# A 256-token encoder layer on one core: q, f, b and up computed in channel rows

## The chip, the core and the metric

The kernel runs on one core of a Trainium2 chip. The core has five engines that work side by side and wait for one another by semaphores: TensorE (matrix products; a pass loads a stationary tile of weights, PEld, and then moves columns past it, PE), VectorE (DVE), ScalarE (ACT), GpSimd (POOL) and SyncE (SP, which here issues the transfers). TensorE writes to PSUM, an accumulator memory of eight banks of 512 fp32 words in each of 128 partitions; the other data lies in SBUF. The metric is the device time of one execution in microseconds, as a median over runs.

## The reference

One layer: a bidirectional HGRN2 mixer, then a gated ConvFFN, each between two RMS norms, on 256 tokens of 2048 channels.

```python
h = rmsnorm(x, norm_pre_mix)
q, f_f, f_b, v, g = split(h @ w_in)            # five parts of 2048 columns
q = silu(q); f = lb + (1 - lb) * sigmoid(f_raw); k = 1 - f
S_t = diag(f_t) S_{t-1} + k_t v_t^T;  o_t = S_t^T q_t      # both directions, 16 heads, summed
m = (rmsnorm(o, gnorm) * silu(g)) @ w_out
x = x + rmsnorm(m, norm_post_mix)
h = rmsnorm(x, norm_pre_ffn)
gate, val = split(dwconv3(h @ ffn_w_in))       # 2 x 5632 columns, filter of width 3 over tokens
x = x + rmsnorm((silu(gate) * val) @ ffn_w_out, norm_post_ffn)
```

## The kernel before

**Products.** Every product is split into chunks of 512 output columns: 20 of w_in (four heads' worth of q, f, b, g or v), 4 of w_o, 22 of w_up, 4 of w_dn. Each fp32 operand is split exactly into a high and a low part of type fp32r, and a product is the sum of high x high, high x low and low x high. The activations lie transposed in SBUF (xh and xl, later h2h and h2l: 16 row tiles of 128 channels by 256 tokens). `gemm` takes, for each of 16 row tiles and each of two blocks of 128 tokens, the block's tile of activations as stationary operand and 512 columns of weights as moving operand (lines 173, 176, 177): 16 x 2 x 3 = 96 passes of 512 columns a chunk. The two results, one bank each for 128 tokens x 512 channels, have the tokens in the partitions. A norm's factor per token (rs1, rs2) is there one number per partition, and is applied as the scale of the ScalarE instruction that reads the bank.

**Weights.** SP loads 1 MB at a time (`load`, line 116, three buffers); ScalarE rounds the high part out of it (line 130) and VectorE subtracts it for the low part (line 131), in parts of two row tiles, three parts ahead of TensorE (`prep`).

**Turning the results.** The gates, the scores and the filter over tokens want the channels in the partitions and the tokens along a row. So the chunks of q, f (forward), b (backward) and up are evicted (ScalarE and, for q, VectorE: lines 303, 304, 321, 594) and then turned by `two_tiles`: eight transposes of 128x128 on TensorE (line 196) into PSUM tiles named tp. What follows reads tp: the copy to qT (314), the forget gates (333), the filter (602, 607, 608). g, v, w_o and w_dn are used with the tokens in the partitions.

**Scores and rest.** `do_scores` makes the decayed scores of four heads in seven levels, with fp32 products of 128 columns (lines 374, 394, 419), VectorE and ScalarE working between levels; `do_o` makes the outputs. In the score of level i the moving operand is gathered in runs of 2^i words out of two arrays.

**What sets the order.** Such work is not done at once but put into lists (`soon`, `later`), and `gemm` takes one step of them after each part of a chunk. Within this, a scheduler orders each engine's instructions by a simulated time; an instruction under `keep_in_program_order` stays where the program has it in respect of others so marked and what precedes it. Each engine then runs its list in order. Four PSUM banks (tag pg) hold the results of two chunks at a time; two hold tp and two the scores.

**Start.** x is loaded in pieces of 256, 256, 512, 512 and 512 columns, in between the first weights; `split_x` transposes two row tiles of x at a time (line 257) and splits them. The mean square of x is taken during the second chunk, so rs1 is there before its results are evicted; rs2 is taken at the end of the first up chunk.

Of the kernel before, what the change touches and what calls it, by code (L numbers as in the profile page):

```python
# [18 lines left out]
P = 128  # L19
# [13 lines left out]
# the parts of the first projection, four heads at a time  # L33
# [3 lines left out]
# columns of the packed per-partition parameters  # L37
# [9 lines left out]
def encoder_layer(  # L47
# [34 lines left out]
    mk = const.tile([P, NLEV - 1, P], U8, name="mk")  # L82
# [51 lines left out]

    def flush():
        while soon or later:
            step()

    def gemm(xh, xl, order="plain", need=None, pre=None, mid=None):
# [16 lines left out]
        for s, m in seq:  # L156
            if s == need:
                flush()
            if pre and m == 0:
                pre(s)  # L160
            if order == "head" and s < 4:
                ahead = 4 + m * s
            elif order == "tail" and s >= nsub - 4 - LOOK:
                late = s - (nsub - 4)
                ahead = nsub + (min(0, 2 * late) if late < 0 else late + 1 if m == 0 else 4)
            else:
                ahead = s + (LOOK if ci else 1)
            prep(base + ahead)
            hi, lo = parts[ci, s]
            for j in range(2):  # L170
                k = 2 * s + j
                a, b = xh[:, k, m * P : (m + 1) * P], xl[:, k, m * P : (m + 1) * P]
                mm = nc.tensor.matmul(ps[m], a, hi[:, j, :], start=(k == 0), stop=False)  # L173
                if j == 0 and (order == "head" and s < 4 or order == "tail" and m == 1 and s >= nsub - 4):
                    tc.keep_in_program_order(mm)
                nc.tensor.matmul(ps[m], a, lo[:, j, :], start=False, stop=False)  # L176
# [5 lines left out]
        return ps  # L182

    def rsqrt_mean(dst, ss, n):
        V.tensor_scalar(dst, ss, 1.0 / n, EPS, op0=ALU.mult, op1=ALU.add)
        G.tensor_tensor(dst, dst, mneg[:, : dst.shape[1]], op=ALU.pow)
# [16 lines left out]
    # ------------------------------------------------------------- start up  # L203
    xh = acts.tile([P, KT, T], F32R, name="xh", tag="ah")
    xl = acts.tile([P, KT, T], F32R, name="xl", tag="al")
# [4 lines left out]
    mkf = spool.tile([P, NLEV - 1, P], F32, name="mkf")  # L210
# [17 lines left out]
    def load_rest():  # L228
        nc.sync.dma_start(prm[:, C_CW:], par[:, C_CW:])
        nc.sync.dma_start(mkf, masks.rearrange("p (l t) -> p l t", t=P))  # L230
        V.tensor_copy(mk, mkf)

    # the tensor engine reaches its full clock after some microseconds of work
# [4 lines left out]
    # lower bounds of the forget gates: softmax over the layers, cumulative  # L238
    # sum, minus the first layer's value
# [12 lines left out]
    def split_x(k2):  # L252
# [5 lines left out]
        for j in range(2):  # L258
            k = 2 * k2 + j
            w1 = prm[:, C_PRE + k : C_PRE + k + 1]  # L260
            S.activation(xh[:, k, :], tp[:, j, :], AF.Copy, scale=w1)
        for j in range(2):
# [3 lines left out]
                xl[:, k, :], tp[:, j, :], w1, xh[:, k, :].bitcast(F32), op0=ALU.mult, op1=ALU.subtract  # L266
# [16 lines left out]
    nop = lambda: None  # L283
# [8 lines left out]
    # ------------------------------------------------------- HGRN2, both ways  # L292
    opool = pool(hstack, "oacts", side="right")
    oh = opool.tile([P, KT, T], F32R, name="oh")
    ol = opool.tile([P, KT, T], F32R, name="ol")
# [11 lines left out]

    def do_q(g):
        ps = gemm(xh, xl) if g else ps0
        qn = [nat.tile([P, 512], F32, name="qn", tag="qn") for _ in range(2)]  # L310
        for m in range(2):
            silu_nat(ps, m, qn[m])
        qT = hp.tile([P, HG, T], F32, name="qT", tag="qT")
        two_tiles(lambda i, tp: S.copy(qT[:, 2 * i : 2 * i + 2, :], tp), qn)
        st["q", g] = qT

    def do_f(g, d):
        ps = gemm(xh, xl) if g or d else ps1
# [10 lines left out]
        def put(i, tp):  # L329
            for j in range(2):  # L330
                h = 2 * i + j
                c = d * NH + g * HG + h
                V.tensor_scalar(
                    f[:, h, :], tp[:, j, :], lb1[:, c : c + 1], lb[:, c : c + 1], op0=ALU.mult, op1=ALU.add
# [6 lines left out]
        two_tiles(put, sn, rest)  # L341
# [86 lines left out]
    def do_g(g):  # L428
        ps = gemm(xh, xl)
# [5 lines left out]
    def do_v(g):  # L435
        ps = gemm(xh, xl)
# [5 lines left out]
    def do_o(g):  # L442
# [23 lines left out]
        def put(i, tp):  # L466
            sl = slice(g * HG + 2 * i, g * HG + 2 * i + 2)
            S.activation(oh[:, sl, :], tp, AF.Copy, scale=gn)
            V.scalar_tensor_tensor(ol[:, sl, :], tp, gn, oh[:, sl, :].bitcast(F32), op0=ALU.mult, op1=ALU.subtract)
# [18 lines left out]
    # -------------------------------------------- output projection, residual  # L488
    ps0 = gemm(oh, ol, need=6)
# [10 lines left out]
    def project(xh_, xl_, sfx, ps0, wp, mw, jp, done):  # L500
        """The product of all columns, and the mean square of its rows."""
# [17 lines left out]
        for n in range(4):  # L519
            if n < 3:  # L520
                ps = ps0 if n == 0 else gemm(xh_, xl_)
                take(n, 0, ps)
            else:
                V.tensor_reduce(part, ss.rearrange("p (m q) -> p m q", q=4)[:, :, :3], axis=AX.X, op=ALU.add)
                V.tensor_scalar(part, part, 1.0 / D, EPS, op0=ALU.mult, op1=ALU.add)
                ps = gemm(xh_, xl_, "tail", mid=lambda ps: take(3, 0, ps))
            take(n, 1, ps)

    h2h = acts.tile([P, KT, T], F32R, name="h2h", tag="ah")
    h2l = acts.tile([P, KT, T], F32R, name="h2l", tag="al")  # L530
    ss2, sx2, rs2 = stile(8, "ss2"), stile(2, "sx2"), stile(2, "rs2")

    def mix_done(m, rs):
# [6 lines left out]
        def split(n):  # L540
# [5 lines left out]
            for j in range(4):  # L546
                k = 4 * n + j
                w1 = prm[:, C_PREF + k : C_PREF + k + 1]
                S.activation(h2h[:, k, ms], tp[:, j, :], AF.Copy, scale=w1)
            for j in range(4):  # L550
# [3 lines left out]
                    h2l[:, k, ms], tp[:, j, :], w1, h2h[:, k, ms].bitcast(F32), op0=ALU.mult, op1=ALU.subtract  # L554
# [19 lines left out]
    project(oh, ol, "m", ps0, wp, mw, bpool, mix_done)  # L574
    ps0 = gemm(h2h, h2l, "head")
# [8 lines left out]
    gh = gpool.tile([P, FT, T], F32R, name="gh")  # L584
    gl = gpool.tile([P, FT, T], F32R, name="gl")
# [4 lines left out]
    def up(c, done):  # L590
        ps = gemm(h2h, h2l) if c else ps0
        un = [fn.tile([P, 512], F32, name="un", tag="un") for _ in range(2)]
        for m in range(2):
            S.activation(un[m], ps[m], AF.Copy, scale=rs2[:, m : m + 1])
# [15 lines left out]
        two_tiles(put, un, lambda: done(acc))  # L610

    for j in range(NJ):
# [6 lines left out]
        def val_done(a, gate=gate, j=j):  # L619
            sl = slice(4 * j, 4 * j + 4)  # L620
            V.tensor_tensor(a, gate[0], a, op=ALU.mult)
            S.copy(gh[:, sl, :], a)
            V.tensor_tensor(gl[:, sl, :], a, gh[:, sl, :].bitcast(F32), op=ALU.subtract)
# [3 lines left out]
    ps0 = gemm(gh, gl, need=20)  # L627
# [14 lines left out]
    project(gh, gl, "f", ps0, wp2, fw, dpool, ffn_done)  # L642


def _masks():
# [3 lines left out]
    return mk.astype(np.float32).reshape(P, -1)  # L649
# [52 lines left out]
```

## Time and profile before

| What | us |
|---|---|
| Median of 3 runs (1385.96 to 1387.13) | 1386.12 |
| Span of the profiled execution | 1383.9 |
| TensorE busy in it | 1372.2 |
| VectorE busy | 862.4 |
| ScalarE busy | 684.1 |
| First to last chunk of w_up | 633.5 to 1135.4 |

The span runs from the first to the last instruction of one profiled execution; the runs are timed apart from it, and their median stands 2.2 us above it. A TensorE pass is shown from its start to the end of its results, and passes overlap, so that busy time says whether TensorE ever stood still, and the step from one start to the next says what a pass costs. In the timeline a row has start, length, engine, line, operation, output<-inputs, the moving shape and a count of merged instructions; what ended an idle time before it stands in brackets. In groups of instructions, the columns behind the bars are busy time, mean length and idle time before them with what ended it. The granted TensorE clock is full in the mean (0.998).

### The profile page before, as it was taken

Reading aid. Unit: us, or ns where it says so; the run is one execution under the profiler, and the core shown is the slowest. Engines: PE = TensorE matmul, PEld = TensorE weight load, DVE = VectorE, ACT = ScalarE, POOL = GpSimd, SP = SyncE. Lnnn points to the kernel's source line nnn. Section 1 sums busy time; section 2 is a strip of 40 time slices with the busy share of each in tenths; the row PEclk is TensorE's granted clock in tenths of the full one; section 3 lists DMA queues with packets and bytes.
Section 4 is the critical chain, followed back from the end, with each engine's and each line's share of the span. In section 5 each row is a group of like instructions: output and inputs, shape, how many; then the busy total and the mean of one; then the engine's idle time right before and its main releaser. Section 6 shows DMA issues by size and latency. Waiting matters only on the chain.

```text
span 1383.9 us, 16448 instructions
## 1 busy us (share of the span) xinstructions
PE 1372.2 (99%) x6562; PEld 1148.5 (83%) x6562; DVE 862.4 (62%) x1007; ACT 684.1 (49%) x899; POOL 13.5 (1%) x21
## 2 busy tenths in 40 slices
PE   8999999999999999999999999999999999999997
PEld 7888888888888888888888888888888888888886
DVE  6577657855785776567566565656566656444444
ACT  6644544444444445456555555555555554434342
POOL 0000000000000000000000000000000000000000
PEclk9999999999999999999999999999999999999999
DMA  8553454445444534663555555555555556555552
GB/s 315 183 188 125 149 174 164 149 140 182 165 152 153 174 130 159 242 255 105 188 197 181 194 182 183 183 182 183 185 184 186 184 192 225 186 199 193 185 205 97
DMA packets 36988, 249.08 MB, mean 180 GB/s; under 512 B 4144, under 2 KB 4784, under 8 KB 7472
## 3 DMA queue, kind: packets, MB, share of 16 engines
q1 hardware_dynamic: 36912, 248.04, 51.9%
q8 instruction: 51, 0.84, 0.2%
q14 instruction: 25, 0.20, 0.0%
HBM read 245.93 MB, written 2.10 MB: 179 GB/s over the span
## 4 chain that ended last, share of the span: by engine, by line
PE 98%; DMA 1%; issue 0%; SPq 0%; DVE 0%; ACT 0%; DVEq 0%; POOLq 0%; POOL 0%
PE pg L176 30%; PE pg L177 30%; PE pg L173 30%; PE sc L394 4%; PE tp L196 2%; DMA xs<-in_x 1%; PE sc L451 1%; PE sc L419 1%; PE sc L374 1%; PE sc L450 1%; PE tp L545 0%; PE tp L257 0%; DVE fw L639 0%; SPq L116 0%; SPq L213 0%
## 5 line engine op out<-in xcount | busy, mean ns | idle before, releaser
L131 DVE TENSOR_TENSOR wlo<-raw,whi 128x1024 fp32r<-128x1024 f32 (+1 forms) x457 | 557.2, 1221 | 426.1 <-ACT whi L130 425.7
L130 ACT CAST whi<-raw 128x1024 fp32r<-128x1024 f32 (+1 forms) x457 | 479.6, 1051 | 506.8 <-PE pg L177 486.9
L177 PE MATMUL pg<-whi,h2l 128*128 128x512 f32 x704 | 276.3, 392 | 0.0
L176 PE MATMUL pg<-wlo,h2h 128*128 128x512 f32 x704 | 276.2, 392 | 0.0
L173 PE MATMUL pg<-whi,h2h 128*128 128x512 f32 x704 | 276.1, 393 | 0.0
L173 PE MATMUL pg<-whi,xh 128*128 128x512 f32 x640 | 251.6, 395 | 0.0
L177 PE MATMUL pg<-whi,xl 128*128 128x512 f32 x640 | 251.4, 393 | 0.0
L176 PE MATMUL pg<-wlo,xh 128*128 128x512 f32 x640 | 250.9, 392 | 0.0
L177 PEld LDWEIGHTS pg<-whi,h2l 128*128 128x128 f32 x704 | 132.3, 188 | 28.3
L176 PEld LDWEIGHTS pg<-wlo,h2h 128*128 128x128 f32 x704 | 132.3, 188 | 26.2
L173 PEld LDWEIGHTS pg<-whi,h2h 128*128 128x128 f32 x704 | 132.2, 188 | 25.9
L177 PEld LDWEIGHTS pg<-whi,xl 128*128 128x128 f32 x640 | 120.2, 188 | 24.6
L176 PEld LDWEIGHTS pg<-wlo,xh 128*128 128x128 f32 x640 | 120.3, 188 | 23.4 <-DVE wlo L131 0.2
L173 PEld LDWEIGHTS pg<-whi,xh 128*128 128x128 f32 x640 | 120.3, 188 | 23.3
L177 PE MATMUL pg<-whi,gl 128*128 128x512 f32 x352 | 137.0, 389 | 0.0
L173 PE MATMUL pg<-whi,gh 128*128 128x512 f32 x352 | 137.0, 389 | 0.0
L176 PE MATMUL pg<-wlo,gh 128*128 128x512 f32 x352 | 137.0, 389 | 0.0
L176 PEld LDWEIGHTS pg<-wlo,gh 128*128 128x128 f32 x352 | 66.1, 188 | 13.8
L173 PEld LDWEIGHTS pg<-whi,gh 128*128 128x128 f32 x352 | 66.1, 188 | 13.7
L177 PEld LDWEIGHTS pg<-whi,gl 128*128 128x128 f32 x352 | 66.1, 188 | 13.6
L394 PEld LDWEIGHTS sc<-qs,kc 128*128 128x128 f32 x448 | 57.9, 192 | 2.2
L607 DVE SCALAR_TENSOR_TENSOR acc<-tp,prm,acc 128x255 f32<-128x255 f32 x88 | 41.8, 476 | 27.3 <-PE tp L196 27.3
(108 smaller groups left out, 1010.6 us busy)
## 6 DMA issues: line engine op xcount, KB each, us to landing
raw<-in_w_up SPq DMA_DIRECT2D x88, 1024.0 KB, 4.9
raw<-in_w_in SPq DMA_DIRECT2D x78, 1024.0 KB, 4.9
raw<-in_w_dn SPq DMA_DIRECT2D x44, 1024.0 KB, 4.9
raw<-in_w_o SPq DMA_DIRECT2D x16, 1024.0 KB, 4.9
x<-in_x SPq DMA_DIRECT2D x1, 2048.0 KB, 7.6
wp<-in_post SPq DMA_DIRECT2D x2, 1024.0 KB, 5.9
out<-fw SPq DMA_DIRECT2D x8, 256.0 KB, 2.5
xs<-in_x SPq DMA_DIRECT2D x3, 512.0 KB, 10.2
```

Of the source, the lines that this page charges most:

```text
L130: S.copy(hi[:, j], src[:, j])
L131: V.tensor_tensor(lo[:, j], src[:, j], hi[:, j].bitcast(F32), op=ALU.subtract)
L173: mm = nc.tensor.matmul(ps[m], a, hi[:, j, :], start=(k == 0), stop=False)
L176: nc.tensor.matmul(ps[m], a, lo[:, j, :], start=False, stop=False)
L177: nc.tensor.matmul(ps[m], b, hi[:, j, :], start=False, stop=(k == 2 * nsub - 1))
L196: nc.tensor.transpose(tp[:, j, m * P : (m + 1) * P], srcs[m][:, c0 : c0 + P], ident)
L374: nc.tensor.matmul(sc[:, j, :], kc[0][:, h, sl], q[:, h, sl], start=True, stop=True)
L394: nc.tensor.matmul(sc[:, j, :], kc[0][:, h, sl], r, start=True, stop=True)
L419: nc.tensor.matmul(sc[:, h, :], ks[:, d, h, s0 : s0 + P], qs[:, 1 - d, h, t0 : t0 + P], start=True, stop=True)
L450: nc.tensor.matmul(o[:, h, :], Sd[:, 2 * h + b, :], v[:, b, cs], start=True, stop=False)
L451: nc.tensor.matmul(o[:, h, :], So[1 - b][:, h, :], v[:, 1 - b, cs], start=False, stop=True)
L607: V.scalar_tensor_tensor(a[:, 1:T], z[:, 0 : T - 1], cw[0], a[:, 1:T], op0=ALU.mult, op1=ALU.add)
```

## The change

`gemm_t` is a second way to compute a chunk: the weights are the stationary operand, in four tiles of 128 columns, and the activations of all 256 tokens move. For each of 16 row tiles and each of the four column tiles there are three passes of 256 columns (lines 205, 208, 209 of the changed kernel): 192 a chunk. The result has the channels in the partitions and the tokens along a row, in two banks of two column tiles each. All q, f and b chunks and all up chunks but the first use it; g, v, the first up chunk, w_o and w_dn keep `gemm` (now lines 175, 178, 179).

With the tokens along the row, a norm's factor per token is no scale per partition any more. `spread` makes a tile with the 256 factors in every partition, r1 for the first norm and r2 for the second: two products of the broadcast factor with the identity (line 226) and a copy (227). VectorE multiplies the result by it while reading it from PSUM (`each_token`, line 349; the same in `up`). Sigmoid, gates and filter then read SBUF; nothing of these chunks is transposed.

High and low activations share a tile (xx, later hh, oo and gg), the masks come as bytes without a conversion, loaded to another pool and later in SP's queue, and the first and last passes of a chunk in `gemm_t` are kept in program order.

```diff
+    def gemm_t(xx, need=None, pre=None):
...
+        ps = [ps_g.tile([P, 2, T], F32, name="pg", tag="pg") for _ in range(2)]
+        for s in range(nsub):
...
+            prep(base + s + (LOOK if ci else 1))
+            hi, lo = parts[ci, s]
+            for j in range(2):
+                k = 2 * s + j
+                for n in range(4):
+                    z, cs = ps[n // 2][:, n % 2, :], slice(n * P, (n + 1) * P)
+                    mm = nc.tensor.matmul(z, hi[:, j, cs], xx[:, k, 0, :], start=(k == 0 and n % 2 == 0), stop=False)
+                    if k == 0:
+                        tc.keep_in_program_order(mm)
+                    nc.tensor.matmul(z, hi[:, j, cs], xx[:, k, 1, :], start=False, stop=False)
+                    mm = nc.tensor.matmul(
+                        z, lo[:, j, cs], xx[:, k, 0, :], start=False, stop=(k == 2 * nsub - 1 and n % 2 == 1)
+                    )
+                    if k == 2 * nsub - 1:
+                        tc.keep_in_program_order(mm)
+            step()
+        return ps
...
+    def spread(rs, name):
+        tp = ps_t.tile([P, 2, T], F32, name="tp", tag="tp")
+        for m in range(2):
+            a = rs[:, m : m + 1].broadcast_to([P, P])
+            nc.tensor.matmul(tp[:, 0, m * P : (m + 1) * P], a, ident, start=True, stop=True)
+        S.copy(name, tp[:, 0, :])
...
+        soon.extend([nop, lambda: spread(rs1, r1)])
...
-    ps0 = gemm(xh, xl, pre=lambda s: split_x(s + 2) if 2 * s + 4 < KT else None)
+    ps0 = gemm_t(xx, pre=lambda s: split_x(s + 2) if 2 * s + 4 < KT else None)
...
-    ps1 = gemm(xh, xl)
+    ps1 = gemm_t(xx)
...
+    mk = opool.tile([P, NLEV - 1, P], U8, name="mk")
+    nc.sync.dma_start(mk, masks.rearrange("p (l t) -> p l t", t=P))
...
+    def each_token(ps, dst):
+        for i in range(2):
+            z = dst[:, 2 * i : 2 * i + 2, :]
+            V.tensor_tensor(z, ps[i], r1[:, None, :].broadcast_to([P, 2, T]), op=ALU.mult)
...
     def do_q(g):
-        ps = gemm(xh, xl) if g else ps0
-        qn = [nat.tile([P, 512], F32, name="qn", tag="qn") for _ in range(2)]
-        for m in range(2):
-            silu_nat(ps, m, qn[m])
+        ps = gemm_t(xx) if g else ps0
         qT = hp.tile([P, HG, T], F32, name="qT", tag="qT")
-        two_tiles(lambda i, tp: S.copy(qT[:, 2 * i : 2 * i + 2, :], tp), qn)
+        each_token(ps, qT)
+        sg = nat.tile([P, HG, T], F32, name="qn", tag="qn")
+        S.activation(sg, qT, AF.Sigmoid)
+        V.tensor_tensor(qT, qT, sg, op=ALU.mult)
...
     def do_f(g, d):
-        ps = gemm(xh, xl) if g or d else ps1
-        sn = [nat.tile([P, 512], F32, name="qn", tag="qn") for _ in range(2)]
-        for m in range(2):
-            S.activation(sn[m], ps[m], AF.Sigmoid, scale=rs1[:, m : m + 1])
+        ps = gemm_t(xx) if g or d else ps1
+        sn = nat.tile([P, HG, T], F32, name="qn", tag="qn")
+        each_token(ps, sn)
+        S.activation(sn, sn, AF.Sigmoid)
...
-        two_tiles(put, sn, rest)
+        soon.extend([put, rest])
...
     rsqrt_mean(rs2, sx2, D)
+    r2 = const.tile([P, T], F32, name="rt", tag="rt")
+    spread(rs2, r2)
...
     def up(c, done):
-        ps = gemm(h2h, h2l) if c else ps0
-        un = [fn.tile([P, 512], F32, name="un", tag="un") for _ in range(2)]
-        for m in range(2):
-            S.activation(un[m], ps[m], AF.Copy, scale=rs2[:, m : m + 1])
+        ps = gemm_t(hh) if c else ps0
...
-        two_tiles(put, un, lambda: done(acc))
+        if c == 0:
+            un = [fn.tile([P, 512], F32, name="un", tag="un") for _ in range(2)]
+            for m in range(2):
+                S.activation(un[m], ps[m], AF.Copy, scale=rs2[:, m : m + 1])
+            two_tiles(put, un, lambda: done(acc))
+            return
+        z = [fn.tile([P, 2, T], F32, name="un", tag="un") for _ in range(2)]
+        for i in range(2):
+            V.tensor_tensor(z[i], ps[i], r2[:, None, :].broadcast_to([P, 2, T]), op=ALU.mult)
+        soon.extend([lambda: put(0, z[0]), lambda: put(1, z[1]), lambda: done(acc)])
```

On each engine the changed program's rows stand at the places of the prediction that they bear on.

More of the change, by code (lines that the diff above doesn't have):

```diff
@@ L81, in encoder_layer @@
     mneg = const.tile([P, 2 * HG], F32, name="mneg")
-    mk = const.tile([P, NLEV - 1, P], U8, name="mk")
+    r1 = const.tile([P, T], F32, name="rt", tag="rt")
     x_v = x.rearrange("(m p) d -> p m d", p=P)
@@ L133, in prep @@
             at["prep"] += 1
+    nop = lambda: None
     def flush():
@@ L137, in flush, with gemm @@
             step()
-    def gemm(xh, xl, order="plain", need=None, pre=None, mid=None):
+    def gemm(xx, order="plain", need=None, pre=None, mid=None):
         ci = at["chunk"]
@@ L171, in gemm @@
                 k = 2 * s + j
-                a, b = xh[:, k, m * P : (m + 1) * P], xl[:, k, m * P : (m + 1) * P]
+                a, b = (xx[:, k, i, m * P : (m + 1) * P] for i in range(2))
                 mm = nc.tensor.matmul(ps[m], a, hi[:, j, :], start=(k == 0), stop=False)
@@ L182, in gemm @@
         return ps
+    def gemm_t(xx, need=None, pre=None):
+        ci = at["chunk"]
+        at["chunk"] += 1
+        nsub = 2 * chunks[ci][2]
+        base = subs.index((ci, 0))
+        ps = [ps_g.tile([P, 2, T], F32, name="pg", tag="pg") for _ in range(2)]
+        for s in range(nsub):
+            if s == need:
+                flush()
+            if pre:
+                pre(s)
+            prep(base + s + (LOOK if ci else 1))
[15 more added lines that the diff above has]
+        return ps
     def rsqrt_mean(dst, ss, n):
@@ L201, in two_tiles @@
         soon.extend([lambda: one(0), lambda: one(1)])
-    xh = acts.tile([P, KT, T], F32R, name="xh", tag="ah")
-    xl = acts.tile([P, KT, T], F32R, name="xl", tag="al")
+    xx = acts.tile([P, KT, 2, T], F32R, name="xx", tag="xx")
     hstack = ExitStack()
@@ L293, in encoder_layer @@
     opool = pool(hstack, "oacts", side="right")
-    oh = opool.tile([P, KT, T], F32R, name="oh")
-    ol = opool.tile([P, KT, T], F32R, name="ol")
+    oo = opool.tile([P, KT, 2, T], F32R, name="oo")
+    mk = opool.tile([P, NLEV - 1, P], U8, name="mk")
+    nc.sync.dma_start(mk, masks.rearrange("p (l t) -> p l t", t=P))
     rstack = ExitStack()
@@ L327, in do_f, with put @@
         f, kk, qq = st["f", g][:, d], st["k", g][:, d], st["d", g][:, 1 - d]
-        def put(i, tp):
-            for j in range(2):
-                h = 2 * i + j
+        def put():
+            for h in range(HG):
                 c = d * NH + g * HG + h
                 V.tensor_scalar(
-                    f[:, h, :], tp[:, j, :], lb1[:, c : c + 1], lb[:, c : c + 1], op0=ALU.mult, op1=ALU.add
+                    f[:, h, :], sn[:, h, :], lb1[:, c : c + 1], lb[:, c : c + 1], op0=ALU.mult, op1=ALU.add
                 )
@@ L486, in encoder_layer @@
             do_o(g)
-    ps0 = gemm(oh, ol, need=6)
+    ps0 = gemm(oo, need=6)
     rstack.close()
@@ L525, in project @@
                 V.tensor_scalar(part, part, 1.0 / D, EPS, op0=ALU.mult, op1=ALU.add)
-                ps = gemm(xh_, xl_, "tail", mid=lambda ps: take(3, 0, ps))
+                ps = gemm(xx_, "tail", mid=lambda ps: take(3, 0, ps))
             take(n, 1, ps)
-    h2h = acts.tile([P, KT, T], F32R, name="h2h", tag="ah")
-    h2l = acts.tile([P, KT, T], F32R, name="h2l", tag="al")
+    hh = acts.tile([P, KT, 2, T], F32R, name="hh", tag="xx")
     ss2, sx2, rs2 = stile(8, "ss2"), stile(2, "sx2"), stile(2, "rs2")
@@ L548, in split @@
                 w1 = prm[:, C_PREF + k : C_PREF + k + 1]
-                S.activation(h2h[:, k, ms], tp[:, j, :], AF.Copy, scale=w1)
+                S.activation(hh[:, k, 0, ms], tp[:, j, :], AF.Copy, scale=w1)
             for j in range(4):
@@ L553, in split @@
                 V.scalar_tensor_tensor(
-                    h2l[:, k, ms], tp[:, j, :], w1, h2h[:, k, ms].bitcast(F32), op0=ALU.mult, op1=ALU.subtract
+                    hh[:, k, 1, ms], tp[:, j, :], w1, hh[:, k, 0, ms].bitcast(F32), op0=ALU.mult, op1=ALU.subtract
                 )
@@ L573, in encoder_layer @@
     extra.append(bpool)
-    project(oh, ol, "m", ps0, wp, mw, bpool, mix_done)
-    ps0 = gemm(h2h, h2l, "head")
+    project(oo, "m", ps0, wp, mw, bpool, mix_done)
+    ps0 = gemm(hh, "head")
     flush()
@@ L583, in encoder_layer @@
     gpool = pool(ctx, "gpool")
-    gh = gpool.tile([P, FT, T], F32R, name="gh")
-    gl = gpool.tile([P, FT, T], F32R, name="gl")
+    gg = gpool.tile([P, FT, 2, T], F32R, name="gg")
     cstack = ExitStack()
```

32 lines of the change are left out of this document (15 added, 17 removed).

## The prediction

> **What bounds the kernel now.** I read the page's busy times and its chain of waits first, then a stretch of whole chunks, then single passes in the timeline.
>
> ```profile
> PE 1372.2 (99%) x6562; PEld 1148.5 (83%) x6562; DVE 862.4 (62%) x1007; ACT 684.1 (49%) x899; POOL 13.5 (1%) x21
> ...
> PE 98%; DMA 1%; issue 0%; SPq 0%; DVE 0%; ACT 0%; DVEq 0%; POOLq 0%; POOL 0%
> ```
>
> TensorE carries 98% of the chain that ended last, so the time is the sum of what TensorE issues. The next view is busy time in a stretch of twenty up chunks (columns: PE, PEld, DVE, ACT, POOL, each with its count, clock, DMA share, GB/s).
>
> ```profile
> 680.83:1135.44 454.61, 454.61 (x2081) 375.18 (x2080) 283.39 (x340) 243.37 (x300) 0.00 (x0) 1.00 0.54 185
> ```
>
> 2080 passes are 20 times 96 matmuls and 8 transposes: 454.61/20 = 22.73 us a chunk. How fast the passes follow one another, and when each one's weights are loaded (PEld), stands in the timeline:
>
> ```profile
> 700.13 0.39 PE L173 MATMUL pg<-whi,h2h 128*128 128x512 f32 x1
> 700.13 0.19 PEld L176 LDWEIGHTS pg<-wlo,h2h 128*128 128x128 f32 x1
> 700.35 0.39 PE L176 MATMUL pg<-wlo,h2h 128*128 128x512 f32 x1
> ...
> 705.57 0.39 PE L173 MATMUL pg<-whi,h2h 128*128 128x512 f32 x1
> ```
>
> From 700.13 to 705.57 there are 24 steps: 226.7 ns each. The 0.39 is the span of one pass, which overlaps the next; the step is the price. The load of the next pass starts with the running pass and hides under it. So 96 matmuls are 21.76 us, and the 8 transposes cost the rest, 0.97 us, or 121 ns each with their change-overs.
>
> **The change part by part.** Removed: 8 transposes in each of 33 chunks (12 of q, f and b, 21 of up). Replaced: 96 passes of 512 columns by 192 of 256 in the same chunks. As many columns move in all, but there are 3168 more passes, each with a load: the counts above are 6562 for PE and PEld alike, though L173 and L176 share their stationary tile, so sharing saves no load, nor will it for L205 and L208. Hence, with p for the step of a 256-column pass, the chunks change by 33 x (192 p - 22.73 us).
>
> The trace has no 256-column pass. Its nearest rows are in the chain of waits (start, length, count) and, for loads not held back by a long pass, in the timeline:
>
> ```profile
> 55.69 0.87 PE tp L196 x8
> ...
> 103.77 2.66 PE sc L394 x16
> ...
> 113.70 1.93 PE sc L394 x16
> ...
> 121.32 1.78 PE sc L394 x16
> ```
> ```profile
> 8.29 0.19 PEld L173 LDWEIGHTS pg<-whi,xh 128*128 128x128 f32 x1
> 8.32 0.48 PE L173 MATMUL pg<-whi,xh 128*128 128x512 f32 x1
> 8.40 0.19 PEld L176 LDWEIGHTS pg<-wlo,xh 128*128 128x128 f32 x1
> ```
>
> Passes of 128 columns step at 108.8 ns (transposes) and 111.3 (scores, 1.78/16). A score's moving operand is cut into runs of words; runs of two give 1.93/16 = 120.6, single words 166. Two loads follow one another at 8.29 and 8.40, 0.11 us apart. So 128-column passes seem to go at about the pace of the loads.
>
> Bounds of p: below, 108.8, since nothing that loads its own weights steps faster. Above, the straight line through 128 columns (111.3) and 512 (226.7): 0.30 ns a column, 73 ns a pass, p = 150 (+203 us on the chunks). That line takes the 128-column rows as set by their columns, and the loads speak against it, so p lies well below. If a pass cost nothing beside its columns, p were 113.3, half of 226.7. What it costs beside them I take from the two-word scores: they too load new weights of four-byte words, and take their moving words in 64 short pieces at the pace of the loads. I take p = 120, which makes some 13 of the 226.7 fixed per pass. Then a chunk is 23.04 us, 0.31 more than before: 33 x 0.31 = +10.2 us. The transposes' 32 us go, 42 us come for twice the passes.
>
> On TensorE, in the middle of the up chunks, the rows before (un is an evicted chunk, waiting to be transposed):
>
> ```order
> L176 MATMUL pg<-wlo,h2h 128x512
> L196 MATMUL tp<-ident,un 128x128
> L177 MATMUL pg<-whi,h2l 128x512
> L173 MATMUL pg<-whi,h2h 128x512
> L176 MATMUL pg<-wlo,h2h 128x512
> L177 MATMUL pg<-whi,h2l 128x512
> L173 MATMUL pg<-whi,h2h 128x512
> L196 MATMUL tp<-ident,un 128x128 x3
> ```
>
> and now:
>
> ```order
> L205 MATMUL pg<-hh,whi 128x256
> L208 MATMUL pg<-hh,whi 128x256
> L209 MATMUL pg<-hh,wlo 128x256
> L205 MATMUL pg<-hh,whi 128x256
> L208 MATMUL pg<-hh,whi 128x256
> ```
>
> The transposes are gone, and weights and activations have changed places.
>
> *The start.* The first passes of each new product are pinned to program order, which moves them on TensorE behind the input transposes. Before (xs is the input, loaded in pieces):
>
> ```order
> L257 MATMUL tp<-ident,xs 128x128 x8
> L173 MATMUL pg<-whi,xh 128x512
> L176 MATMUL pg<-wlo,xh 128x512
> L173 MATMUL pg<-whi,xh 128x512
> L176 MATMUL pg<-wlo,xh 128x512
> ```
>
> now:
>
> ```order
> L294 MATMUL tp<-ident,xs 128x128 x12
> L205 MATMUL pg<-xx,whi 128x256
> L208 MATMUL pg<-xx,whi 128x256
> L209 MATMUL pg<-xx,wlo 128x256
> L205 MATMUL pg<-xx,whi 128x256
> ```
>
> Transposes 9 to 12 read the third piece of x, and every pass now queues behind them. The old start, from the timeline and the chain:
>
> ```profile
> 7.93 0.63 PE L257 MATMUL tp<-ident,xs 128*128 128x128 f32 x4 [1.81 <-DMA xs<-in_x]
> ...
> 11.15 0.61 PE L173 MATMUL pg<-whi,xh 128*128 128x512 f32 x2
> 12.31 1.06 PE L257 MATMUL tp<-ident,xs 128*128 128x128 f32 x8 [0.55 <-DMA xs<-in_x]
> ```
> ```profile
> 4.09 8.09 DMA xs<-in_x
> ```
>
> The third piece lands at 12.18. Before, 14 passes ran between 8.32 and 11.6; now TensorE stands still there: 14 x 0.227 = +3.2 us. It would be nothing if the piece came by 8.3, but its transfer's place in the queue is unchanged.
>
> *Spread.* r1 and r2 take two fp32 products each, which count twice in the trace (L394 has 448 rows for 224 products): 8 passes of 111 ns, +0.9 us. r1 was ready long before. r2 stands on TensorE right behind the first up chunk and holds all passes of the second:
>
>
> ```profile
> 658.13 0.61 PE L173 MATMUL pg<-whi,h2h 128*128 128x512 f32 x2
> ```
> ```profile
> 658.51 1.27 ACT L594 ACTIVATE un<-pg,rs 128x512 f32<-128x512 f32 x2 [1.85 <-POOL rs L186]
> ```
>
> The second chunk began at 658.13 and the row means were ready at 658.51: +0.5 us with the hand-over; between 0 and 2.
>
> *Other engines, at nothing.* Scaling by token moves to DVE, two multiplications a chunk out of PSUM, as L515 does:
>
> ```profile
> L515 DVE TENSOR_TENSOR mw<-pg,wp 128x512 f32<-128x512 f32 x8 | 5.4, 685 | 1.1 <-ACT jk L510 1.1
> ...
> L339 DVE TENSOR_TENSOR qs<-qT,f 128x1024 f32<-128x1024 f32 x8 | 9.7, 1218 | 0.0
> ```
>
> That is 1.4 us in a chunk of 22.7, in which DVE works 283.39/20 = 14.2 us; ACT's two evictions go, and filters and gates read SBUF in place of PSUM. A q chunk adds at most one multiplication over 1024 columns more (1.22, as L339). TensorE's 22.7 us cover it, and the accumulators of two chunks fit at a time. If it did not, and every chunk waited for its 1.4, it were 33 x 1.4 = 46 us. The mask load moves behind the last reader of x on SP's queue, with weight loads behind it: taken as 0, since weights are loaded several parts ahead; at worst some 2 us, once.
>
> Sum: +10.2 +3.2 +0.9 +0.5 = +14.8 us on the profiled 1383.9, whose run lies 2.2 below the median of 1386.1: 1398.7, and **1401 us** as a median. The change breaks even at 192 p = 22.73 - 4.6/33, p = 117.7 ns.
>
> **Rivals.**
> *Columns alone set the step* (p = 113.3). For it: the step of 226.7 is the same over 24 passes, and no row shows a stop between two passes of this type. Against it: the two-word scores. 33 x (21.75 - 22.73) = -32.3, +4.6: 1358 us, faster.
>
> *The loads' own pace sets the step* (p = 109 to 111.3). For it: the rows at 128 columns and 8.29/8.40. Against it: half of 226.7 is already more. At 111.3: 33 x (21.37 - 22.73) = -44.9, +4.6: 1346; at 109 1331. The Trainium skill, TensorE: Matmul & The Clock Gate, Back-to-back issue gap, gives columns/2.4 + 2.5 ns; 256 columns would then step at an estimated 109.2, and the time be 1333. By that rule 512 columns step at 215.8; the trace has 226.7.
>
> *The load shows* (p = 125 and up). A load of 0.11 us that starts with the running pass ends after about as long as 256 columns take, and if the fixed 13 ns begins only then, p = 111 + 13, some 125: 33 x (24.00 - 22.73) = +41.9, +4.6: 1433 us. It decides from the point where a pass is shorter than a load and its hand-over. For it: nothing of these 0.11 us had to hide so tightly before. Against it: the 128-column rows keep 111 with a load each. At its end no load hides at all: p = 113 + 109 = 222, +657 us, 2043. That is what the Trainium skill's rule makes of it, in the same page's part on packing, The mechanism: a load overlaps running matmuls only when it goes to other row groups. The trace denies it: at 700.13 load and pass of all 128 rows run together and the step stays 226.7.
>
> **How the numbers follow.** My forecast (p 118.5 to 122, 1393 to 1408 us) has 0.57, columns alone 0.20, the loads' pace 0.09, the load showing 0.09 (0.01 of it for no hiding), and 0.05 lies between forecast and columns, near break-even. Faster by over 0.2% (about what a measurement of this kernel tells from no change, 2.8 us) is 0.30, within 0.05, slower 0.65. The range reaches from 1350, under the columns' case, to 1412: it holds 0.82. The forecast's own range is 1393 to 1408.
>
> **What would show it.** The step between L205, L208 and L209: 120 ns right, 113 or 109 to 111 the first two rivals, 125 the third. A middle up chunk: 23.04 us against 22.73. The first L205 after 12.4 us. An idle TensorE of about half a microsecond ahead of the second spread, none elsewhere; if DVE or ACT release TensorE inside the chunks, the cover was too thin. If the step is under 117.7 ns, the sign of the forecast is wrong.

## The result, and the profile after

The changed kernel takes 1408.97 us as a median (1405.46 to 1410.01), the kernel before, run beside it, 1386.04 (1385.88 to 1387.13). The ratio is 1.0158, its 95% interval 1.0142 to 1.0174: slower by 23 us, where the forecast was slower by 15. The profiled execution took 1408.33, its span is 1406.5, 22.6 above the 1383.9 of before.

The page of the changed kernel has the busy times and the chain of waits:

```profile
PE 1388.6 (99%) x9474; PEld 1295.5 (92%) x9474; DVE 897.8 (64%) x1068; ACT 652.7 (46%) x839; POOL 13.5 (1%) x21
...
PE 97%; ACT 1%; issue 1%; DVE 1%; DMA 1%; SPq 0%; POOL 0%; DVEq 0%; POOLq 0%; ACTq 0%
PE pg L209 18%; PE pg L205 18%; PE pg L208 18%; PE pg L178 12%; PE pg L175 12%; PE pg L179 12%; PE sc L436 4%; PE sc L493 1%; PE sc L461 1%; PE sc L492 1%; PE sc L416 1%; DMA xs<-in_x 1%; PE tp L237 0%; ACT hh L592 0%; ACT jk L604 0%
```

TensorE still carries the chain, and the three lines of passes of 256 columns are 54% of it. How fast they follow one another stands in its timeline in the middle of the up chunks, the passes first and then the loads:

```profile
799.80 0.28 PE L205 MATMUL pg<-hh,whi 128*128 128x256 f32 x1
799.92 0.28 PE L208 MATMUL pg<-hh,whi 128*128 128x256 f32 x1
800.04 0.28 PE L209 MATMUL pg<-hh,wlo 128*128 128x256 f32 x1
...
801.00 0.28 PE L208 MATMUL pg<-hh,whi 128*128 128x256 f32 x1
```
```profile
799.92 0.19 PEld L209 LDWEIGHTS pg<-hh,wlo 128*128 128x128 f32 x1
800.04 0.19 PEld L205 LDWEIGHTS pg<-hh,whi 128*128 128x128 f32 x1
```

From 799.80 to 801.00 are ten steps: 120.0 ns each. The load of a pass starts with the pass before it, also every 120 ns. Busy time by stretch, for twenty up chunks, gives the same (columns as before: PE, PEld, DVE, ACT, POOL, clock, DMA share, GB/s):

```profile
675.20:1136.00 460.80, 460.80 (x3843) 460.80 (x3842) 306.89 (x379) 220.20 (x262) 0.00 (x0) 1.00 0.52 183
```

460.80/20 = 23.04 us a chunk, where it was 22.73. VectorE has 15.3 us of work in a chunk (306.89/20), ScalarE 11.0, and TensorE never stands still.

Where the 22.6 us came from can be read from the starts of the chunks' first passes in both timelines:

| Stretch | Before, us | After, us | Difference |
|---|---|---|---|
| To the first pass of the first chunk | 8.32 | 12.01 | +3.7 |
| First chunk | 25.44 | 27.63 | +2.2 |
| Other 19 chunks of w_in | 505.40 | 516.62 | +11.2 |
| w_o and the first up chunk | 118.97 | 118.05 | -0.9 |
| 21 up chunks | 477.31 | 484.77 | +7.5 |
| w_dn and the end | 248.46 | 247.42 | -1.0 |

The last up chunk's eight transposes used to run behind the start of w_dn, and so their 0.97 us are missing there. The 21 up chunks took the first up chunk's transposes in both kernels: 21 x 0.31 + 0.97 = 7.5. Of the two middle rows, 1.8 us have only changed places: 16 score passes of the last group (`sc<-qs,ks`) ran beside w_o before and now run ahead of it. The first three rows hold more than the passes. At the start, the timeline of the changed kernel:

```profile
5.25 1.06 PE L294 MATMUL tp<-ident,xs 128*128 128x128 f32 x4
8.65 1.09 PE L294 MATMUL tp<-ident,xs 128*128 128x128 f32 x4 [2.34 <-DMA xs<-in_x]
11.27 1.09 PE L294 MATMUL tp<-ident,xs 128*128 128x128 f32 x4 [1.53 <-DMA xs<-in_x]
12.01 0.56 PE L205 MATMUL pg<-xx,whi 128*128 128x256 f32 x1
12.37 0.41 PE L208 MATMUL pg<-xx,whi 128*128 128x256 f32 x1
...
17.06 0.41 PE L209 MATMUL pg<-xx,wlo 128*128 128x256 f32 x1
...
17.87 0.28 PE L208 MATMUL pg<-xx,whi 128*128 128x256 f32 x1
17.99 0.28 PE L209 MATMUL pg<-xx,wlo 128*128 128x256 f32 x1
```

The first pass stands behind the transposes of the third piece of x, as the prediction said. The 22 steps from 12.37 to 17.06 take 213 ns each, and only from 17.87 on do they take 120. That is TensorE at half its rate. In this trace it had that rate before the idle times already: the four transposes at 5.25 and at 8.65 take 1.06 and 1.09 us, where the kernel before has 0.87 and 0.63 (at 5.26 and 7.93).

The views of what TensorE waited for (us in total, times, longest) and its timeline near 390 us show a second place:

```profile
PE sc L436 <- DVE qs L443: 4.5, 2, 3.1
PE tp L294 <- DMA xs<-in_x: 3.9, 2, 2.3
...
```
```profile
386.15 3.57 PE L436 MATMUL sc<-qs,kc 128*128 128x128 f32 x16 [3.13 <-DVE qs L443]
391.13 2.02 PE L436 MATMUL sc<-qs,kc 128*128 128x128 f32 x16 [1.41 <-DVE qs L443]
392.91 0.36 PE L205 MATMUL pg<-xx,whi 128*128 128x256 f32 x1
```

Just behind the first of these waits, busy time by stretch has the clock column (the third from the end) at half:

```profile
386.00:389.40 3.40, 3.25 (x15) 3.28 (x16) 2.47 (x4) 0.00 (x0) 0.00 (x0) 0.50 0.73 292
```

In the kernel before, the same levels of the third head group's scores (now L436, there L394) stood with some 6 us of passes between two of them, in its timeline:

```profile
371.71 1.50 PE L394 MATMUL sc<-qs,kc 128*128 128x128 f32 x8
...
380.32 2.09 PE L394 MATMUL sc<-qs,kc 128*128 128x128 f32 x16
...
387.94 1.95 PE L394 MATMUL sc<-qs,kc 128*128 128x128 f32 x16
```

A level needs queries that VectorE has decayed after the level before (L443). Now the first pass of the next chunk, q of the fourth group, is pinned behind these levels, so nothing lies between them: TensorE waits 4.5 us for VectorE, and its clock falls to half in the meantime. In the first two groups the chunk that follows g is v, which isn't pinned; there the passes still lie between.

### The profile page after: what moved, and what is told of

Its sections match the earlier page's. It is cut to its first block, busy times and chain, and to the rows that moved or that the text cites. A ratio compares the mean times of both kernels' runs of the same rounds, so it can differ in the third digit from the quotient of the medians.

```text
span 1406.5 us, 22359 instructions
## 1 busy us (share of the span) xinstructions
PE 1388.6 (99%) x9474; PEld 1295.5 (92%) x9474; DVE 897.8 (64%) x1068; ACT 652.7 (46%) x839; POOL 13.5 (1%) x21
## 4 chain that ended last, share of the span: by engine, by line
PE 97%; ACT 1%; issue 1%; DVE 1%; DMA 1%; SPq 0%; POOL 0%; DVEq 0%; POOLq 0%; ACTq 0%
PE pg L209 18%; PE pg L205 18%; PE pg L208 18%; PE pg L178 12%; PE pg L175 12%; PE pg L179 12%; PE sc L436 4%; PE sc L493 1%; PE sc L461 1%; PE sc L492 1%; PE sc L416 1%; DMA xs<-in_x 1%; PE tp L237 0%; ACT hh L592 0%; ACT jk L604 0%
## 5 line engine op out<-in xcount | busy, mean ns | idle before, releaser
L205 PE MATMUL pg<-hh,whi 128*128 128x256 f32 x1344 | 380.6, 283 | 0.0
L208 PE MATMUL pg<-hh,whi 128*128 128x256 f32 x1344 | 380.4, 283 | 0.0
L209 PE MATMUL pg<-hh,wlo 128*128 128x256 f32 x1344 | 380.3, 283 | 0.0
L208 PEld LDWEIGHTS pg<-hh,whi 128*128 128x128 f32 x1344 | 258.0, 192 | 0.0
L209 PEld LDWEIGHTS pg<-hh,wlo 128*128 128x128 f32 x1344 | 258.0, 192 | 0.0
L205 PEld LDWEIGHTS pg<-hh,whi 128*128 128x128 f32 x1344 | 258.0, 192 | 0.0
L205 PE MATMUL pg<-xx,whi 128*128 128x256 f32 x768 | 219.9, 286 | 0.0
L208 PE MATMUL pg<-xx,whi 128*128 128x256 f32 x768 | 218.7, 285 | 0.0
L209 PE MATMUL pg<-xx,wlo 128*128 128x256 f32 x768 | 218.6, 285 | 0.0
L208 PEld LDWEIGHTS pg<-xx,whi 128*128 128x128 f32 x768 | 148.4, 193 | 0.1
L205 PEld LDWEIGHTS pg<-xx,whi 128*128 128x128 f32 x768 | 148.4, 193 | 0.1
L209 PEld LDWEIGHTS pg<-xx,wlo 128*128 128x128 f32 x768 | 148.2, 193 | 0.0
L175 PE MATMUL pg<-whi,gg 128*128 128x512 f32 x352 | 136.9, 389 | 0.0
L179 PE MATMUL pg<-whi,gg 128*128 128x512 f32 x352 | 136.9, 389 | 0.0
L175 PE MATMUL pg<-whi,xx 128*128 128x512 f32 x256 | 100.5, 395 | 0.0
L179 PE MATMUL pg<-whi,xx 128*128 128x512 f32 x256 | 100.4, 392 | 0.0
```

What stands on the lines that cost most here:

```text
L205: mm = nc.tensor.matmul(z, hi[:, j, cs], xx[:, k, 0, :], start=(k == 0 and n % 2 == 0), stop=False)
L208: nc.tensor.matmul(z, hi[:, j, cs], xx[:, k, 1, :], start=False, stop=False)
L209: mm = nc.tensor.matmul(z, lo[:, j, cs], xx[:, k, 0, :], start=False, stop=(k == 2 * nsub - 1 and n % 2 == 1))
```

## The experiments

The theory after the comparison: the pass of 256 columns costs 120.0 ns, 13.3 ns beside its columns, and accounts for some 12 of the 23 us with the products of `spread`; the pin of a chunk's first pass accounts for the rest, at two places. The rivals: the rest comes from the work in channel rows itself (VectorE's added multiplications near the scores, the order that they force), and, for the pass, the 120 ns are the pace of the loads and not a price beside the columns.

**The first pass of a chunk set free.**

```diff
-                    if k == 0:
+                    if k == 0 and n:
                         tc.keep_in_program_order(mm)
```

> The changed kernel with one thing undone: the very first pass of a chunk in channel rows may again be put ahead of the work before it (the other pins stay). Theory A (the part of the +23 us that the 120 ns step does not explain is the pin: 5.9 us at the start, where passes wait behind the third piece of x and then run at half clock, and some 7 us in the third group of heads, where three score levels follow one another with no passes between): both go, about 1396 us (1393 to 1399). Theory B (the third group's wait comes from VectorE's added multiplications, whatever the order): only the start goes, 1402 to 1406.

Measured: 1399.04 us (1396.12 to 1399.39), ratio to before 1.0087 (1.0072 to 1.0102), span 1394.3. Its timeline and its waits:

```profile
8.12 0.36 PE L205 MATMUL pg<-xx,whi 128*128 128x256 f32 x1
8.85 0.39 PE L208 MATMUL pg<-xx,whi 128*128 128x256 f32 x1 [0.37 <-DVE xx L302]
9.07 0.28 PE L209 MATMUL pg<-xx,wlo 128*128 128x256 f32 x1
...
377.80 2.09 PE L436 MATMUL sc<-qs,kc 128*128 128x128 f32 x16
...
384.15 1.95 PE L436 MATMUL sc<-qs,kc 128*128 128x128 f32 x16
```
```profile
PE tp L294 <- DMA xs<-in_x: 1.4, 1, 1.4
...
PE pg L208 <- DVE xx L302: 0.4, 1, 0.4
```

The first pass is back at 8.12, its successors step at 120 ns from 9.07 on, the levels have their passes between them again, and no wait for qs is left. The chunks and all work in channel rows are as in the changed kernel, so the rest of the 23 us isn't theirs: 10 us hang on this one pin, by the medians. (The spans differ by 12.2, but the profiled execution is the fastest of these four runs.) With 1399.04 the time is at the upper bound of theory A. The other 19 chunks of w_in take 510.06 us where the changed kernel takes 516.62, so the second place alone is 6.6.

**The pin alone**, in the kernel before: products, transposes and evictions are untouched.

```diff
+                if k == 0 and m == 0 and (ci < 20 and ORDER[ci][0] in "qfb" or ci > C_UP and ci < C_UP + 2 * NJ):
+                    tc.keep_in_program_order(mm)
```

> The kernel before, with only the pin added: the first pass of every q, f and b chunk and of every up chunk but the first stays behind the TensorE instruction ahead of it in the program; all passes are of 512 columns and all transposes stay. Theory A: the start loses 3 to 6 us, and the third group of heads, where four score levels now follow one another, 5 to 12: 1394 to 1404 us. Theory B: only the start, 1389 to 1392.

Measured: 1397.22 us (1396.53 to 1398.01), ratio 1.0080 (1.0063 to 1.0097), span 1394.8. Its timeline in the third group:

```profile
373.36 2.82 PE L396 MATMUL sc<-qs,kc 128*128 128x128 f32 x16
...
378.08 3.21 PE L396 MATMUL sc<-qs,kc 128*128 128x128 f32 x16 [1.91 <-DVE qs L403]
...
382.70 3.40 PE L396 MATMUL sc<-qs,kc 128*128 128x128 f32 x16 [1.41 <-DVE qs L403]
...
387.51 2.02 PE L396 MATMUL sc<-qs,kc 128*128 128x128 f32 x16 [1.41 <-DVE qs L403]
```

Without one pass of 256 columns, the pin costs 11 us at the same two places: the second chunk starts 3.0 us later than before (36.76 against 33.76), and the stretch from the chunk of g in the third group to w_o takes 7.9 us more (201.12 against 193.26). From w_o on nothing is added: the first chunk of w_o starts 10.82 us later than before, that of w_dn 10.83. So what stalls the third group is the order, and not VectorE's added work.

**One half of the change at a time.** First the up chunks alone in channel rows, with q, f and b left as before:

```diff
-    ps0 = gemm_t(xx, pre=lambda s: split_x(s + 2) if 2 * s + 4 < KT else None)
+    ps0 = gemm(xx, pre=lambda s: split_x(s + 2) if 2 * s + 4 < KT else None)
...
-    ps1 = gemm_t(xx)
+    ps1 = gemm(xx)
...
-        each_token(ps, qT)
...
+        two_tiles(lambda i, tp: S.copy(qT[:, 2 * i : 2 * i + 2, :], tp), qn)
...
```

> Only up in channel rows; q, f and b as before, with transposes. Both theories: 21 chunks of 23.04 in place of 22.73 us, +6.5, and +1.1 for spread and the wait for the second norm's factor: 1393.5 us (1392 to 1395). Above 1397 a part of the unexplained time lies in up.

Measured: 1394.58 us (1394.25 to 1395.92), ratio 1.0061 (1.0046 to 1.0076). The 21 chunks from 659.94 to 1144.72 take 484.78 us, the 484.77 of the whole change; TensorE has no wait in the third group. Then q, f and b alone, up left as before:

```diff
-    r2 = const.tile([P, T], F32, name="rt", tag="rt")
-    spread(rs2, r2)
...
-        ps = gemm_t(hh) if c else ps0
+        ps = gemm(hh) if c else ps0
...
```

> Only q, f and b in channel rows; up as before, with transposes. Theory A: 12 chunks x 0.31 = +3.7, start +5.9, third group +7, spread +0.5: 1403 us (1400 to 1405). With the run of up alone the two additions make up the whole +23.

Measured: 1403.24 us (1401.66 to 1404.43), ratio 1.0121 (1.0106 to 1.0136). Its waits for qs are those of the whole change:

```profile
PE tp L294 <- DMA xs<-in_x: 5.3, 2, 3.6
PE sc L436 <- DVE qs L443: 4.5, 2, 3.1
```

The halves add 8.4 and 17.0 us to the 1386.22 of the kernel before beside them, 25.4 together, 2.5 more than the whole; by the spans the sum is some 4.7 above the whole. Of these, 4.1 have a place in the traces. In the run with q, f and b the wait for x is 5.3 us where the whole change waits 3.9, its first pass comes at 13.45 and its second chunk 0.95 us later; its third group takes 2.2 us more, with the clock at half for 10.2 us (386.3 to 396.6) in place of 3.4. In the run with up alone the start takes 1.0 us more than in the kernel before, with 3.4 us at half clock (8.9 to 12.3), though no first pass is pinned there. So both places vary from run to run by a microsecond or two, and the clock with them. Both pinned places lie in the half with q, f and b.

**What a pass costs by its columns.** In three of the up chunks the same stationary weights are met by 128, 384 or 512 columns; these three chunks so don't give their product.

```diff
+                    w = {5: 128, 9: 384, 13: 512}.get(ci - C_UP)
...
+                    if w:
+                        xw = xx[:, k].rearrange("p a b -> p (a b)")[:, :w]
+                        for h in range(3):
...
+                                ps[n // 2] if z0 else zw, (lo if h > 1 else hi)[:, j, cs], xx[:, k] if z0 else xw,
...
```

> The changed kernel, in which three up chunks move other widths past the same stationary weights: the sixth 128 columns (384 passes), the tenth 384 and the fourteenth 512 (192 passes each); what these three chunks give is not the product, so the output differs. The steps of the passes are the measure. Theory A (13.3 ns a pass and 0.4167 ns a column, and a load needs about 110 of its own): 384 columns 173 ns, 512 columns 227, 128 columns 109 to 112, the load's pace in place of 67. Rival (the 13 ns belong to the short pass, since its load hides less): 384 columns 160 to 168. Rival (loads hide at any width): 128 columns 67.

Measured in a single run (1458.94 us in all). Its timeline in the three chunks:

```profile
769.78 0.28 PE L209 MATMUL pg<-hh,wlo 128*128 128x128 f32 x1
769.89 0.61 PE L209 MATMUL pg<-hh,whi 128*128 128x128 f32 x4
770.34 0.38 PE L209 MATMUL pg<-hh,wlo 128*128 128x128 f32 x2
```
```profile
880.97 0.51 PE L222 MATMUL pg<-hh,whi 128*128 128x384 f32 x2
881.32 0.33 PE L222 MATMUL pg<-hh,wlo 128*128 128x384 f32 x1
...
882.01 0.51 PE L222 MATMUL pg<-hh,whi 128*128 128x384 f32 x2
```
```profile
984.77 0.39 PE L222 MATMUL pg<-hh,whi 128*128 128x512 f32 x1
...
986.36 0.39 PE L222 MATMUL pg<-hh,wlo 128*128 128x512 f32 x1
```

Five steps of 128 columns from 769.78 to 770.34 are 112 ns each, six of 384 from 880.97 to 882.01 are 173 ns, seven of 512 from 984.77 to 986.36 are 227 ns. With 120 at 256 these lie on 13.3 ns + columns x 0.4167 ns: 120.0, 173.3, 226.7. At 128 that line gives 66.7, and the trace 112, the pace of the loads. Neither rival holds: the one has 160 to 168 at 384 columns, the other 67 at 128. So 120 is on the line of the columns, 8 ns above the loads: 256 columns is the narrowest of these widths that pays for its columns. The fixed 13.3 is there at 512 too, once per pass; the change pays it twice as often.

**Fewer passes instead of transposes.** If the 13.3 ns per pass are what the change pays, the channel rows can be had with fewer passes: the high weights meet high and low activations in one pass of 512 columns (they share a tile), the low weights meet the high activations in 256. Per row tile and 128 weight columns that is 226.7 + 120.0 = 346.7 ns in place of 3 x 120.0. A bank's two halves are then added at the eviction (a copy on ScalarE, an addition and the multiplication on VectorE). Here it is done in the up chunks, with q, f and b as before and nothing pinned.

```diff
+    def gemm_p(xx, take):
...
+                for n in range(2):
+                    cs = slice(n * P, (n + 1) * P)
+                    nc.tensor.matmul(ps[n], hi[:, j, cs], xx[:, k], start=(k == 0), stop=False)
+                    nc.tensor.matmul(ps[n][:, 0, :], lo[:, j, cs], xx[:, k, 0, :], start=False, stop=(k == KT - 1))
...
+                S.copy(z[i][:, n, :], ps[n][:, 1, :])
+                V.tensor_tensor(z[i][:, n, :], ps[n][:, 0, :], z[i][:, n, :], op=ALU.add)
+            V.tensor_tensor(z[i], z[i], r2[:, None, :].broadcast_to([P, 2, T]), op=ALU.mult)
...
```

> q, f and b as before; up in channel rows, 256 columns of weights at a time in four banks a chunk: the high weights meet high and low activations in one pass of 512 columns (64 a chunk), the low weights the high activations in one of 256 (64 a chunk); a copy and an addition join the two halves at the eviction, nothing is pinned. Theory A (13.3 ns a pass, whatever is stationary): a chunk is 64 x 226.7 + 64 x 120.0 ns = 22.19 us against 22.73 before, 21 x -0.54 = -11.3, spread and its wait +1.1: 1376 us (1374 to 1379). Rival (the added copy, addition and multiplication, some 5 us a chunk on ScalarE and VectorE, hold the banks and stop TensorE): 1386 or more.

Measured: 1384.51 us (1383.08 to 1384.9), ratio 0.9982 (0.9972 to 0.9991), span 1382.9. It is under both kernels, but gains 2 us on the kernel before (1386.52 beside it) and not 10: neither expectation holds. TensorE waits for nothing in the up chunks, so the rival's cause is out; the pairs are longer, in its timeline:

```profile
800.33 0.40 PE L201 MATMUL pg<-hh,whi 128*128 128x512 f32 x1
800.57 0.28 PE L202 MATMUL pg<-hh,wlo 128*128 128x256 f32 x1
800.69 0.40 PE L201 MATMUL pg<-hh,whi 128*128 128x512 f32 x1
...
805.28 0.40 PE L201 MATMUL pg<-hh,whi 128*128 128x512 f32 x1
```

From 800.33 to 805.28 are 14 pairs of 353.6 ns, 6.9 more than the sum. 64 pairs a chunk and 21 chunks make 9 us of it, which is what is missing.

**The same passes in groups.** Eight passes of 512 and then eight of 256, in place of turns; the edit is against the kernel with joint passes.

```diff
-            for j in range(4):
-                k = 4 * (s % 4) + j
+            ks = [4 * (s % 4) + j for j in range(4)]
+            for j, k in enumerate(ks):
                 for n in range(2):
                     cs = slice(n * P, (n + 1) * P)
                     nc.tensor.matmul(ps[n], hi[:, j, cs], xx[:, k], start=(k == 0), stop=False)
+            for j, k in enumerate(ks):
+                for n in range(2):
+                    cs = slice(n * P, (n + 1) * P)
                     nc.tensor.matmul(ps[n][:, 0, :], lo[:, j, cs], xx[:, k, 0, :], start=False, stop=(k == KT - 1))
```

> The same computation as the kernel with joint passes of 512 columns, with the up passes in another order: for each part of four row tiles first the eight joint passes of 512 columns, then the eight passes of 256 columns of the low weights. Before, joint and low passes took turns, and a pair took 353.5 ns in place of 226.7 + 120.0 = 346.7. A: the taking of turns costs the 6.8 ns (a short pass between two long ones); in groups the steps are 226.7 and 120.0 but at the two change-overs of a part, an up chunk is about 22.2 us, and the time 1376 (1373 to 1379). B: the 6.8 ns come with a second reading of the same weights' neighbours or with the evictions beside the passes, wherever these stand: the steps in groups still add to some 353 a pair and the time stays at 1384 (1382 to 1387).

Measured: 1379.62 us (1377.82 to 1380.99) against 1385.14 of the kernel before beside it, ratio 0.9958 (0.9941 to 0.9975), span 1378.0: the fastest of all. Its timeline:

```profile
800.75 2.00 PE L201 MATMUL pg<-hh,whi 128*128 128x512 f32 x8
802.60 1.11 PE L205 MATMUL pg<-hh,wlo 128*128 128x256 f32 x8
803.55 2.00 PE L201 MATMUL pg<-hh,whi 128*128 128x512 f32 x8
```

Eight passes of 256 take 0.95 us, 119 ns each; eight of 512 take 1.85, 231 ns each, 4 more than 226.7. A pair is now 350 ns. So the taking of turns did cost, and half of it goes with the groups; neither expectation has it whole, and the time lies 0.6 us above the first one's bound. Single starts in the trace place the excess: of the steps of such a group of 512, the first five (800.755 to 801.916) take 232 ns in the mean, the last three (to 802.596) 227. So it stands behind the change from 256 to 512 and fades; why stays open.

## Why the prediction was right, and where it wasn't

The time of 1408.97 us is inside the wide range, 1350 to 1412, and 1 us above the forecast's own, 1393 to 1408. Slower was right, and so was the price of a pass; the terms for the pin were 8 us too small.

**The price of a pass was right, and the way to it was luck in part.** The forecast stood on p = 120, against the columns alone (113.3), the loads (109 to 111.3) and a load that shows (125 and up); the trace has 120.0, and the chunk its 23.04 us. Some 13 ns beside the columns are now measured at three widths, 256, 384 and 512. But the two-word scores, from which they were taken, don't show them: scores with longer runs take 111.3 ns at the same 128 columns, and at 128 columns the pass runs at the loads' pace, so that the scores' 9 ns more go with the runs of two words. That they led to the same 120 is chance. Of the rivals, the loads' pace holds where the columns are fewer: 112 ns at 128. The rule of the Trainium skill (TensorE: Matmul & The Clock Gate, Back-to-back issue gap), given there for an isolated matmul, puts the fixed part at 2.5 ns; the trace has 13.3 here.

Three figures of the working don't follow from its own sum: the straight line's p = 150 puts 199 us on the chunks (203 is with the 4.6 of the other terms), no hiding at all gives 2047 (2043 is without them), and p from 118.5 to 122 gives 1391 to 1414 and not 1393 to 1408.

**The up chunks were right to a tenth**: 21 x 0.31 and the 0.97 of the first one's transposes give the measured 7.5 us. So was the wait ahead of the second `spread`, in the timeline of the changed kernel:

```profile
673.22 0.39 PE L179 MATMUL pg<-whi,hh 128*128 128x512 f32 x1
673.85 0.71 PE L226 MATMUL tp<-ident,rs 128*128 128x128 f32 x4 [0.24 <-POOL rs L219]
```

From 673.22 the next pass would have come at 673.45, and it comes at 673.85: 0.4 us, where 0.5 was said.

**"Other engines, at nothing" was right inside the chunks**: VectorE's 15.3 us and ScalarE's 11.0 lie under 23.04, and with the first pass free no wait for either is left but 0.4 us at the start. The chunks of that kernel add up from the rows alone. A chunk's passes cost 192 x 120.0 - 96 x 226.7 ns = 1.28 us more. The other 19 chunks of w_in take 4.66 us more than before (510.06 against 505.40): 11 x 1.28 for the passes, less 12 x 0.97 for the transposes, 0.44 for the first `spread` and 1.78 for the 16 score passes that ran beside w_o before make 4.66. Its 21 up chunks take 7.8 us more (485.14 against 477.31): 7.5 as above, and 0.4 for the second `spread`, which lies in this stretch when the first pass may go ahead of it.

**The step "The start" was mis-sized.** The third piece of x holds the passes back, as predicted: the first comes at 12.01 (12.4 was said), 3.7 us later. But the step then let them run at full rate. They ran 22 steps at 213 in place of 120 ns, 2.0 us. With the 2.2 of the first chunk the start takes 5.9 us more; 1.3 of these are what that chunk's own passes cost, which the forecast has among its chunks, so the term is 4.6 us and not 3.2. The clock column of this stretch doesn't show the half rate. The run with other widths begins in the same way, with 20 steps of 213 ns from 12.43 to 16.70, and there busy time by stretch has the clock at 0.50:

```profile
12.40:16.90 4.50, 4.50 (x23) 4.50 (x22) 3.24 (x4) 2.72 (x4) 0.00 (x0) 0.50 1.06 416
```

How far the start varies can be read from the other traces. With the first pass pinned in channel rows the second chunk begins at 39.6 to 40.6 us (three traces), with the first pass free at 33.8 to 35.4 (five traces, the kernel before among them).

**One place of the pin was not followed at all**, and it is most of the error. The prediction says that "the first passes of each new product are pinned", and followed this only where x arrives. The same pin stands ahead of q of the fourth group, where the passes of that chunk had been the cover of VectorE's work between two levels of scores: 4.5 us of waiting and a level at half clock, 6.6 us by the run with the first pass free. Its own list of signs would have led astray here: "if DVE or ACT release TensorE inside the chunks, the cover was too thin". DVE does release it, but VectorE had become no slower (its multiplication into qs takes 1223 ns in the mean, before 1225); the pinned order had taken the cover away, as the pin alone shows in the kernel before.

Together: +14.8 was forecast; 1.4 more at the start and 6.6 in the third group make 22.8, and the trace has 22.6.

## What to carry to other kernels

A pass of 256 to 512 columns cost its columns and 13.3 ns here: halving the columns doubles that fixed part, which can eat the transposes saved; operands that share a tile can win it back, when one wide pass does the work of two. A pin that keeps an instruction in program order must be followed at every place that it holds, and most of all where the instructions behind it had been the cover of a chain between two engines. When an engine releases another in the trace, look first at what lay in that gap before, and only then at the engine's own work.

## What was not expected of the hardware

At half rate the fixed part of a pass doesn't show: with the clock column at 0.50, 256 columns step at 213 ns, just twice the 106.7 that 256 columns come to at 0.4167 ns each. That agrees with the Trainium skill (TensorE: Matmul & The Clock Gate, Back-to-back issue gap), which has the columns alone at half clock.

In the changed kernel a wait of 3.13 us was enough for TensorE's clock to fall to 0.50 for 3.4 us (386.0 to 389.4), and a level of 16 passes took 3.57 us there in place of 1.95. In the kernel before with the pin alone, a wait of 1.91 us that ended at 378.08 was followed by half clock for longer:

```profile
378.80:385.60 6.80, 5.39 (x26) 5.13 (x25) 5.24 (x6) 1.04 (x1) 0.00 (x0) 0.50 0.31 128
```

So such a wait can cost more than its own length.

Passes of 512 and 256 columns in turns take 353.6 ns a pair and 350 in groups of eight, where the two steps by themselves add up to 346.7; no run here shows why.
